# Every second tile of the ada stream on GpSimd, in a sum of its own

## Chip, cores, metric

The kernel runs on 1 core of one Trainium2 chip. The metric is the device time of one execution in microseconds (us), from which the median of several runs is taken. The core has five engines with a queue each: TensorE (PE in the profile; its weight loads are PEld), VectorE (DVE), ScalarE (ACT), GpSimd (POOL) and SyncE (SP), which here only issues DMAs.

## The reference

One layer of a decoder: 512 tokens of width 2048, in float32. A vector `c` gives, through one large matrix, six rows of 2048 values that shift, scale and gate the two halves of the layer:

```python
mod = (silu(c) @ w_ada + b_ada)                 # w_ada: 2048 x 12288
sh_a, sc_a, gt_a, sh_f, sc_f, gt_f = split(mod, 6)
h = rms_norm(x, g_attn) * (1 + sc_a) + sh_a
y = parallel_mixers(h, ...)                     # one projection w_in, two attentions, two gates, w_o
x = x + gt_a * y
h = rms_norm(x, g_ffn) * (1 + sc_f) + sh_f
x = x + gt_f * conv_ffn(h, ...)                 # w_up, 3-tap causal convolution, silu gate, w_down
```

Mixer A is an attention over the 128 keys that an indexer selects for each query; mixer B is a dense causal attention with latent projections (w_mq_up, w_mkv_up). Their outputs go through w_pa and w_pb, are multiplied by the sigmoids of the two gates, added, and go through w_o.

## The kernel before

**Products.** Every weight is used as two parts, high and low (`split`, lines 137 to 139, and `wtile`, lines 117 to 135): ScalarE rounds the float32 tile to its high part, VectorE subtracts that from the tile for the low part, and TensorE makes three products for each pair of operands (`mm3`, lines 141 to 144). A weight tile is 128 x 1024 in most places. It arrives in one of 5 buffers of `raw` by a DMA of SyncE's queue; its two parts stand in one of 3 pairs of buffers of `whl`. Part of the gates, nearly all of w_up, and w_down are multiplied by a scheme of seven products of halves instead of eight (`seven`, lines 948 to 1085; its matmuls are lines 1077 to 1079, its additions of weights line 973, its additions out of PSUM line 985).

**The ada stream.** The first two rows of `mod` are made at the start (`ada_units`). The other four, 8192 values, are made beside all the work from the mixer's attention to w_o, by `ada_stream` (lines 727 to 758), a generator. It has 16 blocks of 512 columns. A block has 16 tiles of 128 x 512 of `w_ada`; each is multiplied by one column of `c_act` (a scalar for each partition) and added to the block's sum `acc`, one of three tiles. One step of the generator handles a pair of tiles. The work around it asks for steps by a `ticker`: a rate for each stage (one step per weight tile in the gates beside attention A, 0.36 per step of the seven products, 1.25 per weight tile in w_pa, w_pb and w_o).

**Where a tile lands.** The load of a pair goes, in SyncE's queue, to one of three places: two tiles of the common pool (attention A and the gates; line 736), a `raw` buffer of the weights (from the first w_mkv_up to the last w_pa; line 740), or a ring of six pool tiles (w_pb and w_o; line 736 too). The pool has 81 tiles of 128 x 512 (`get`, `put`); a tile is given back as soon as the instructions that use it are recorded, and the next user waits for them. SyncE's queue is worked off in order.

**The end of a block.** `pend` keeps the finished sums. `flush_cols` (lines 780 to 797) splits each, adds its 128 partitions by two matmuls with a matrix of ones (lines 785 and 786) and stores the row or takes its columns. It is called at the beginning of a block of products, or when a sum is over three steps old.

**Order.** The kernel is recorded in one order; a scheduler of the build then orders the instructions of each engine by its own estimates and priorities (the loads and splits of weights have a high one). So an edit can move instructions that it doesn't touch.

**GpSimd before.** It issues the DMAs that store and reload attention outputs and gates (lines 713, 714, 807, 808, 827, 1108, 1109, 1274 to 1276), fills a few tiles with zeros (line 1169), and makes the power -0.5 of the norms, on 1 to 4 columns (`rsqrt_mean`, line 246).

Of the kernel before, what the change touches and what calls it, by code (L numbers as in the profile page):

```python
# [15 lines left out]
ALU = mybir.AluOpType  # L16
# [15 lines left out]
def trunk_layer_kernel(  # L32
# [21 lines left out]
    V, A, G, PE, SP = nc.vector, nc.scalar, nc.gpsimd, nc.tensor, nc.sync  # L54
# [14 lines left out]
    def get(dt=F32):  # L69

        i = min(free, key=lambda n: rested[n])
        free.remove(i)
        if cur[i] is None or cur[i].dtype != dt:
            cur[i] = pool.tile([P, T], dt, name=f"slot{i}", tag=f"slot{i}")
        held[id(cur[i])] = i
        return cur[i]
# [4 lines left out]
    def put(*ts, lag=2):  # L81

        for t in ts:
            i = held.pop(id(t))
            rested[i] = clock[0] + lag
            free.append(i)
# [146 lines left out]
    c_act = pool.tile([P, KD], F32, name="c_act")  # L233
# [312 lines left out]
    for tb in range(1, 4):  # L546
# [12 lines left out]
        acc = get()  # L559
        rl = [get(), get(), get()]  # L560
        for hd in range(16):
# [9 lines left out]
            else:  # L571
                V.scalar_tensor_tensor(acc[:, :S], r[:, :S], wi[:, tb, hd:hd + 1], acc[:, :S],  # L572
                                       op0=ALU.mult, op1=ALU.add)
# [146 lines left out]
    ada_blocks = [8, 9, 10, 11, 16, 17, 18, 19, 12, 13, 14, 15, 20, 21, 22, 23]  # L720
    gst = [get(), get()]
    ada_acc = [get(), get(), get()]

    ada_in_slots = [False]
    ada_ring_on, ada_ring = [False], deque()

    def ada_stream():
        for n, cb in enumerate(ada_blocks):
            assert len(pend) < 3
            acc = ada_acc[n % 3]  # L730
            for kp in range(8):
                if ada_in_slots[0]:
                    ts = [ada_ring.popleft(), ada_ring.popleft()] if ada_ring else [get(), get()]
                    for i in range(2):
                        k = kp * 2 + i
                        SP.dma_start(ts[i], w_ada[k * P:(k + 1) * P, cb * 512:(cb + 1) * 512])
                else:
                    raw = rawq.popleft()
                    t = raw[:, 0:1024].rearrange("p (k n) -> p k n", k=2)
                    SP.dma_start(t, w_ada[kp * 2 * P:(kp + 1) * 2 * P, cb * 512:(cb + 1) * 512]  # L740
                                 .rearrange("(k p) n -> p k n", p=P))
                    ts = [t[:, 0], t[:, 1]]
                for i in range(2):
                    k = kp * 2 + i
                    if k == 0:
                        V.tensor_scalar(acc, ts[i], c_act[:, 0:1], None, op0=ALU.mult)
                    else:
                        V.scalar_tensor_tensor(acc, ts[i], c_act[:, k:k + 1], acc,  # L748
                                               op0=ALU.mult, op1=ALU.add)
                if ada_ring_on[0]:  # L750
                    ada_ring.extend(ts)
                elif ada_in_slots[0]:
                    put(*ts)
                else:
                    rawq.append(raw)
                yield None
            pend.append((cb, acc))
            done[0] += 1

    pend = []  # L760
    done = [0]
    stream = ada_stream()

    credit = [0.0]
# [326 lines left out]
    for i in range(KH // 2):  # L1091
        raw = [get() for _ in range(4)]
        ta, tb_ = get(), get()
        for j in range(2):
            k, o = 2 * i + j, slice(j * HT, (j + 1) * HT)
# [334 lines left out]
    def up_group(grp):  # L1430
        gt = []

        def ev_g(m, b):
            t = conv(grp * 4 + m, b)
            A.activation(t, t, AF.Silu)
            gt.append(t)

        bk = half()
        flush_cols(bk[3])
        lin_fm(w_up, grp * 512, h2, KD, bk, ev_g, tick=sum_tick)  # L1440

        def ev_v(m, b):
            t = conv(44 + grp * 4 + m, b)
            V.tensor_tensor(t, t, gt[m], ALU.mult)
            f_out(grp * 4 + m, t)
            put(gt[m])

        lin_fm(w_up, 512 + grp * 512, h2, KD, half(), ev_v, tick=sum_tick)

    put(*ada_acc)  # L1450
    up_group(0)

    def ffn_out(i):
# [186 lines left out]
```

## Time and profile before

| | |
|---|---|
| median of 3 runs | 2657.04 us (2654.15 to 2658.64) |
| profiled execution | 2656.78 us, its span 2655.0 us |
| TensorE busy | 2588.7 us, 98% |
| VectorE busy | 2174.6 us, 82% |
| ScalarE busy | 1243.0 us, 47% |
| GpSimd busy | 365.8 us, 14% |

The profile is of one execution. The span runs from its first instruction to its last. An engine is busy while one of its instructions runs; waiting and issuing DMAs from SyncE is not counted, and TensorE's matmuls overlap, so that its busy time is the time in which at least one runs. In a row of a group, the number behind x is the count, the next the busy time in us, then the mean ns of one, then the engine's idle time just before, and who ended it. In a row of waits stand the waiting engine and line, an arrow to what it waited for, the us in total, the times and the longest. In a row of the timeline stand the start in us from the span's beginning, the duration in us, engine, line, operation, tiles and shapes.

### The profile page before, as it was taken

How to read it: one execution, taken by the hardware profiler on the slowest of the kernel's cores; microseconds unless marked ns; L12 is line 12 of the kernel's file. 1: busy time of each engine (PE TensorE's matmuls, PEld its weight loads, DVE VectorE, ACT ScalarE, POOL GpSimd, SP SyncE). 2: the span in 40 equal slices, each digit the busy share in tenths (PEclk: the TensorE clock that was granted, in tenths of full speed). 3: DMA queues.
4: the chain of work that ended last, by engine and by line, in shares of the span. 5: the costliest groups of instructions: out<-in, count | busy, mean ns of one | idle time of the engine just before them, and what ended most of it. 6: DMA issues, size and time to landing. Idle time of an engine off the chain costs nothing.

```text
span 2655.0 us, 44904 instructions
## 1 busy us (share of the span) xinstructions
PE 2588.7 (98%) x17168; PEld 2344.2 (88%) x17168; DVE 2174.6 (82%) x3491; ACT 1243.0 (47%) x1953; POOL 365.8 (14%) x671
## 2 busy tenths in 40 slices
PE   6999999999999999999999999999999999999999
PEld 5777687778998877888789999999999999999999
DVE  7886975779878786983669899899899889878787
ACT  4333434334445544322544555555555556655454
POOL 1000011010023223200100000000001024413120
PEclk8999899999999999999999999999999999999999
DMA  9953136774676489873324434433434447867563
GB/s 342 340 165 101 35 101 192 224 215 150 203 240 190 153 274 354 299 238 95 135 74 143 135 124 129 137 123 129 136 123 150 142 146 217 219 155 202 143 208 114
DMA packets 215661, 464.31 MB, mean 175 GB/s; under 512 B 23786, under 2 KB 65156, under 8 KB 215444
## 3 DMA queue, kind: packets, MB, share of 16 engines
q1 hardware_dynamic: 170260, 344.93, 40.4%
q0 software_dynamic: 45152, 116.50, 15.0%
q8 instruction: 134, 2.20, 0.3%
q14 instruction: 83, 0.68, 0.1%
q10 hardware_dynamic: 32, 0.01, 0.0%
HBM read 397.11 MB, written 64.23 MB: 174 GB/s over the span
## 4 chain that ended last, share of the span: by engine, by line
PE 80%; issue 7%; DMA 6%; DVE 5%; ACT 1%; POOL 1%; SPq 0%; POOLq 0%; DVEq 0%; ACTq 0%
PE bank L1077 15%; PE bank L1079 15%; PE bank L1078 15%; PE bank L142 10%; PE bank L143 10%; PE bank L144 10%; DMA slot<-in_w_ada 3%; DVE whl L139 1%; DMA x<-slot 1%; PE bank L708 1%; PE bank L903 1%; DVE slot L572 0%; DMA raw<-in_w_ada 0%; PE bank L700 0%; DMA slot<-in_x 0%
## 5 line engine op out<-in xcount | busy, mean ns | idle before, releaser
L1077 PE MATMUL bank<-slot,whl 128*128 128x256 f32 x3920 | 1102.7, 282 | 21.0 <-ACT slot L977 6.1
L1078 PE MATMUL bank<-slot,whl 128*128 128x256 f32 x3920 | 1098.9, 281 | 0.2 <-DVE slot L139 0.2
L1079 PE MATMUL bank<-slot,whl 128*128 128x256 f32 x3920 | 1088.2, 281 | 6.0 <-DVE whl L139 6.0
L138 ACT ACTIVATE whl<-raw 128x1024 fp32r<-128x1024 f32 (+2 forms) x560 | 532.6, 953 | 618.2 <-PE bank L1078 400.7
L1077 PEld LDWEIGHTS bank<-slot,whl 128*128 128x128 f32 x3920 | 738.9, 189 | 28.2 <-ACT slot L977 8.6
L1078 PEld LDWEIGHTS bank<-slot,whl 128*128 128x128 f32 x3920 | 740.1, 189 | 0.6 <-DVE slot L139 0.5
L1079 PEld LDWEIGHTS bank<-slot,whl 128*128 128x128 f32 x3920 | 732.3, 188 | 7.2 <-DVE whl L139 7.2
L139 DVE TENSOR_TENSOR whl<-raw,whl 128x1024 fp32r<-128x1024 f32 (+2 forms) x560 | 606.0, 1087 | 121.2 <-ACT whl L138 116.9
L130 ACT ACTIVATE whl<-raw 128x1024 fp32r<-128x1024 f32 (+4 forms) x182 | 187.3, 1031 | 385.6 <-PE bank L144 193.8
L973 DVE TENSOR_TENSOR raw<-raw 128x1024 f32<-128x1024 f32 (+2 forms) x320 | 347.3, 1085 | 6.7 <-DMA raw<-in_w_ups 3.7
L131 DVE TENSOR_TENSOR whl<-raw,whl 128x1024 fp32r<-128x1024 f32 (+4 forms) x182 | 215.8, 1186 | 163.7 <-ACT whl L130 162.7
L143 PE MATMUL bank<-whl,slot 128*128 128x512 f32 (+2 forms) x768 | 297.3, 388 | 0.9 <-DVE whl L131 0.9
L142 PE MATMUL bank<-whl,slot 128*128 128x512 f32 (+2 forms) x768 | 293.1, 393 | 4.3 <-ACT slot L409 3.8
L144 PE MATMUL bank<-whl,slot 128*128 128x512 f32 (+2 forms) x768 | 292.9, 385 | 0.0
L142 PE MATMUL bank<-slot,whl 128*128 128x512 f32 (+1 forms) x656 | 264.1, 407 | 6.2 <-DVE slot L703 3.8
L143 PE MATMUL bank<-slot,whl 128*128 128x512 f32 (+1 forms) x656 | 266.0, 406 | 0.1
L144 PE MATMUL bank<-slot,whl 128*128 128x512 f32 (+1 forms) x656 | 258.0, 402 | 0.0
L748 DVE SCALAR_TENSOR_TENSOR slot<-slot,c_act,slot 128x512 f32<-128x512 f32 x203 | 150.9, 747 | 46.0 <-DMA slot<-in_w_ada 44.4
L142 PEld LDWEIGHTS bank<-whl,slot 128*128 128x128 f32 x768 | 146.0, 190 | 35.6 <-ACT slot L409 3.9
L143 PEld LDWEIGHTS bank<-whl,slot 128*128 128x128 f32 x768 | 146.3, 191 | 30.0 <-DVE whl L131 1.4
L144 PEld LDWEIGHTS bank<-whl,slot 128*128 128x128 f32 x768 | 144.7, 189 | 29.4 <-issue 0.5
L142 PEld LDWEIGHTS bank<-slot,whl 128*128 128x128 f32 (+1 forms) x656 | 123.7, 189 | 37.2 <-DVE slot L703 4.2
(288 smaller groups left out, 2705.5 us busy)
## 6 DMA issues: line engine op xcount, KB each, us to landing
slot<-in_w_ada SPq DMA_DIRECT2D x344, 256.0 KB, 5.4
raw<-in_w_ups SPq DMA_DIRECT2D x160, 512.0 KB, 5.1
raw<-in_w_in SPq DMA_DIRECT2D x50, 512.0 KB, 3.7
raw<-in_w_down SPq DMA_DIRECT2D x64, 384.0 KB, 3.8
raw<-in_w_down SPq DMA_DIRECT2D x64, 320.0 KB, 3.1
slot<-f POOLq DMA_DIRECT2D x154, 128.0 KB, 4.1
f<-slot POOLq DMA_DIRECT2D x66, 256.0 KB, 5.1
raw<-in_w_gs SPq DMA_DIRECT2D x32, 512.0 KB, 3.9
```

The lines of the kernel that those rows point to most:

```text
L130: A.activation(hi, raw[:, :w], AF.Copy)
L131: V.tensor_tensor(lo, raw[:, :w], r32(hi), ALU.subtract)
L138: A.activation(dst_hi, src, AF.Copy)
L139: V.tensor_tensor(dst_lo, src, r32(dst_hi), ALU.subtract)
L142: PE.matmul(o, lh, rh, start=first, stop=False)
L143: PE.matmul(o, lh, rl, start=False, stop=False)
L144: PE.matmul(o, ll, rh, start=False, stop=last)
L748: V.scalar_tensor_tensor(acc, ts[i], c_act[:, k:k + 1], acc, op0=ALU.mult, op1=ALU.add)
L973: V.tensor_tensor(o[:, :W], a[:, :W], b[:, :W], op)
L1077: PE.matmul(o, wh[:, ks], rh, start=first and k == 0, stop=False, skip_group_check=True)
L1078: PE.matmul(o, wh[:, ks], rl, start=False, stop=False, skip_group_check=True)
L1079: PE.matmul(o, wl[:, ks], rh, start=False, stop=last, skip_group_check=True)
```

## The change

In each pair of tiles the second one goes to GpSimd. GpSimd multiplies it by its scalar, in place, and adds it to a sum of its own, `acc_g`; the first odd tile of a block is multiplied straight into `acc_g`. VectorE keeps the first tile of each pair with its fused multiplication and addition. At the end of a block VectorE adds `acc_g` to `acc`. There are two tiles `acc_g`, used in turn and taken from the pool with the other sums, given back with them.

```diff
     ada_acc = [get(), get(), get()]
+    ada_acc_g = [get(), get()]
...
-            acc = ada_acc[n % 3]
+            acc, acc_g = ada_acc[n % 3], ada_acc_g[n % 2]
...
                 for i in range(2):
                     k = kp * 2 + i
-                    if k == 0:
-                        V.tensor_scalar(acc, ts[i], c_act[:, 0:1], None, op0=ALU.mult)
+                    if i:
+                        G.tensor_scalar(ts[i] if kp else acc_g, ts[i], c_act[:, k:k + 1], None, op0=ALU.mult)
+                        if kp:
+                            G.tensor_tensor(acc_g, acc_g, ts[i], ALU.add)
+                    elif kp == 0:
+                        V.tensor_scalar(acc, ts[i], c_act[:, k:k + 1], None, op0=ALU.mult)
                     else:
                         V.scalar_tensor_tensor(acc, ts[i], c_act[:, k:k + 1], acc,
                                                op0=ALU.mult, op1=ALU.add)
...
+            V.tensor_tensor(acc, acc, acc_g, ALU.add)
             pend.append((cb, acc))
...
-    put(*ada_acc)
+    put(*ada_acc, *ada_acc_g)
```

The multiplication of GpSimd is line 748 of the changed kernel, its addition line 750, VectorE's first and other tiles lines 752 and 754, the addition of the two sums line 763; the lines behind are shifted by seven, those ahead of line 722 not at all.

## Prediction

> **What bounds the kernel now.** I read the engines' shares and the chain that ended last first, then the busy time by stretches, cut where the work around the ada stream changes, then what TensorE waited for.
>
> ```profile
> span 2655.0 us, 44904 instructions
> ...
> PE 2588.7 (98%) x17168; PEld 2344.2 (88%) x17168; DVE 2174.6 (82%) x3491; ACT 1243.0 (47%) x1953; POOL 365.8 (14%) x671
> ...
> PE 80%; issue 7%; DMA 6%; DVE 5%; ACT 1%; POOL 1%; SPq 0%; POOLq 0%; DVEq 0%; ACTq 0%
> ```
>
> TensorE bounds the kernel. VectorE, which the change relieves, is second, and 5% of the chain. GpSimd is nearly idle.
>
> ```profile
> core 0: us, PE busy (x) PEld busy (x) DVE busy (x) ACT busy (x) POOL busy (x), PEclk, DMA share, GB/s
> 440.00:590.00 150.00, 150.00 (x671) 116.41 (x670) 116.16 (x252) 55.68 (x115) 13.97 (x26) 1.00 0.71 222
> 590.00:660.00 70.00, 64.22 (x415) 57.77 (x414) 64.33 (x95) 29.42 (x41) 4.84 (x9) 0.95 0.52 169
> 660.00:790.00 130.00, 126.66 (x1044) 125.56 (x1044) 108.22 (x124) 54.39 (x71) 17.27 (x33) 0.99 0.66 208
> 790.00:960.00 170.00, 169.57 (x831) 138.47 (x830) 132.11 (x408) 87.04 (x193) 46.49 (x69) 1.00 0.61 189
> 960.00:1060.00 100.00, 95.12 (x402) 72.25 (x401) 75.18 (x141) 40.85 (x76) 30.58 (x57) 0.97 0.98 345
> 1060.00:1200.00 140.00, 140.00 (x602) 112.78 (x602) 121.06 (x173) 48.02 (x69) 18.96 (x32) 1.00 0.78 259
> 1200.00:1330.00 130.00, 126.97 (x573) 102.67 (x573) 66.08 (x98) 50.19 (x77) 9.62 (x17) 0.99 0.33 114
> ```
>
> The second column is TensorE's busy time, the fourth VectorE's, the sixth GpSimd's. The ada stream runs from 440 to 1200 us. In those six stretches TensorE is idle for 0 + 5.8 + 3.3 + 0.4 + 4.9 + 0 = 14.4 us. No relief of VectorE can bring more than that: 0.54% of the time. The waits of TensorE from 440 to 1330 us say whose fault it was:
>
> ```profile
> PE bank L142 <- DVE slot L703: 3.8, 1, 3.8
> PE bank L1077 <- ACT slot L138: 3.5, 1, 3.5
> PE bank L1079 <- DVE whl L139: 3.3, 2, 2.7
> PE bank L1077 <- ACT slot L826: 2.1, 1, 2.1
> PE bank L700 <- DVE slot L692: 0.9, 1, 0.9
> ```
>
> The two waits of L1077 (5.6 us) fall at the start of the gate products in halves, where VectorE is 92% busy (64.33 of 70) making their operands; L139 is VectorE's half of the split of weights. So VectorE is the limit for some 9 us, around 590 to 790 us. The 3.8 us of L703 is a copy out of PSUM in the attention's end.
>
> **What leaves VectorE.**
>
> ```profile
> L748 DVE SCALAR_TENSOR_TENSOR slot<-slot,c_act,slot 128x512 f32<-128x512 f32 x203 | 150.9, 747 | 46.0 <-DMA slot<-in_w_ada 44.4
> L139 DVE TENSOR_TENSOR slot<-slot,slot x148: 406/683/694, 474.0 to 2543.4; 128x512 fp32r<-128x512 f32 x134, 128x256 fp32r<-128x256 f32 x14
> ```
>
> The stream has 16 blocks of 16 tiles. The 8 odd tiles of each go: 128 x 0.747 = 95.6 us. One add of two 128x512 tiles per block comes, at the 0.683 us median of the like-shaped split: 16 x 0.683 = 10.9 us. VectorE loses 84.7 us, almost all of it where TensorE has work anyway.
>
> **What GpSimd gets.** 128 multiplications, 112 additions of 128x512; no such operation is in the trace. The nearest rows:
>
> ```profile
> L1169 POOL MEMSET slot<- 64x512 f32 x8 | 4.2, 524 | 9.4 <-PE bank L1209 5.7 <-PE bank L1078 2.2 <-PE bank L1213 0.7
> masks.py:199 POOL TENSOR_SCALAR_AFFINE_SELECT ident<-ident 128x128 f32<-128x128 f32 x1 | 0.3, 312 | 0.1
> L192 POOL MEMSET mhalf<- 128x4 f32 x1 | 0.1, 102 | 0.0
> ```
>
> A fill of 512 columns takes 0.52 us; that is the lower end for one input. The select reads and writes 128 columns in 0.312 us, 0.102 of it the fixed cost of the smallest fill; for 512 columns 0.10 + 4 x 0.21 = 0.94 us is the upper end. I take 0.75, between them, as the select compares too. An addition reads twice: 0.10 + 2 x 0.42 = 0.94 us from the fill, 0.10 + 2 x 0.84 = 1.78 us from the select; I take 1.2, nearer the fill, since most of a select's price is not its reading. An odd tile then costs GpSimd 1.95 us (1.46 to 2.72) where VectorE paid 0.75. In all 128 x 0.75 + 112 x 1.2 = 230 us, on an engine with time for it.
>
> The Trainium skill, "GPSIMD Engine Reference", section 3.1, has about 2.6 cycles per element at 1.2 GHz for two inputs, by which I estimate 512 x 2.6 / 1.2 = 1.1 us for an addition; the sum would be nearly the same.
>
> **What that does to VectorE.** GpSimd's only reading operation in the stream's time is the small power L246, and the trace shows it beside VectorE's splits:
>
> ```profile
> 817.83 0.70 POOL L246 TENSOR_TENSOR rs<-rsm,mhalf 128x2 f32<-128x2 f32 x1 [1.70 <-DVE rsm L245]
> 805.18 0.95 DVE L131 TENSOR_TENSOR whl<-raw,whl 128x768 fp32r<-128x768 f32 x1
> 805.34 1.33 POOL L246 TENSOR_TENSOR rs<-rsm,mhalf 128x2 f32<-128x2 f32 x1 [0.59 <-DVE rsm L245]
> 813.49 1.21 DVE L131 TENSOR_TENSOR whl<-raw,whl 128x1024 fp32r<-128x1024 f32 x1
> 813.65 1.82 POOL L246 TENSOR_TENSOR rs<-rsm,mhalf 128x2 f32<-128x2 f32 x1 [6.39 <-DVE rsm L245]
> ```
>
> Alone the power takes 0.70 us. Started inside a split it takes 1.33 and 1.82 us: the first ends 0.54 us behind its split (806.67 against 806.13). The two engines do not read at the same time: GpSimd stood until VectorE's operation was over. That VectorE also stands while GpSimd reads cannot be seen here, as two columns take no time. Bounds for VectorE: nothing (84.7 us gained), or the whole of GpSimd's 230 us wherever VectorE's operation reads two tiles in SBUF, as the splits, the subtractions L973 and the stream's own L748 do.
>
> The Trainium skill, "SBUF — State Buffer", section "Who interferes with whom", says that such a pair of operations excludes each other for a whole instruction, whichever started first; the trace agrees for GpSimd's side (1.33 and 1.82 against 0.70 us), and no run here shows VectorE's.
>
> I take the upper bound in the gate products and less elsewhere. The stream's operations by stretch (in the same stretches as above; 16 of TENSOR_SCALAR form come on top, so odd tiles are 8/15 of the count):
>
> ```profile
> 440.00:590.00 150.00, 43.70 (x59) 1.00 0.71 222
> 590.00:660.00 70.00, 11.88 (x16) 0.95 0.52 169
> 660.00:790.00 130.00, 20.97 (x28) 0.99 0.66 208
> 960.00:1060.00 100.00, 32.67 (x44) 0.97 0.98 345
> 1060.00:1200.00 140.00, 44.68 (x60) 1.00 0.78 259
> ```
>
> - 590 to 660 us: 8.5 odd tiles. VectorE 64.3 - 8.5 x 0.747 + 0.7 for one add = 58.7; with GpSimd's 8.5 x 1.95 = 16.6 one after the other 75.3 us, in a stretch of 70. VectorE sets the pace there already: **+5 us**.
> - 660 to 790 us: 15 odd tiles. 108.2 - 11.2 + 1.4 + 29.3 = 127.7 of 130 us. The room falls from 22 to 2 us, and a split that comes late stops TensorE (L139, above): **+4 us**, between -3.3 (that wait goes) and +10.
> - 440 to 590 us: 31.5 odd tiles, 116.2 - 23.5 + 2.7 + 61.4 = 157 of 150 us if everything were excluded, but here many of VectorE's operations read PSUM or a single tile (the attention's minima, scalings and copies); TensorE never waited here, and weights are split ahead: 0.
> - 1060 to 1200 us: 32 odd tiles, 121.1 - 23.9 + 2.7 + 62.4 = 162 of 140, with 64 us of VectorE's idle time right behind it and TensorE full in both: 0.
> - 960 to 1060 us: 23.5 odd tiles are 46 us for GpSimd beside its 30.6 us, mostly DMA issues: 76% busy. Stores and reloads of attention outputs and gates stand behind additions that wait for their tile to land (98% of the DMA engines' time is taken here). TensorE already lost 4.9 us here: **+3 us**, from 0 to 8.
> - Relief: of the 9 us of waits on VectorE's load some goes: **-2 us**, at most -9.
>
> **The order of issue.** The stream's loads, the weights' loads and their waits share SyncE's queue (SyncE's waits from 440 to 1330 us; the first row is of the DMA issues).
>
> ```profile
> slot<-in_w_ada SPq DMA_DIRECT2D x344, 256.0 KB, 5.4
> SPq L736 <- DVE slot L748: 86.7, 129, 3.5
> SPq L126 <- DVE whl L131: 226.5, 67, 20.7
> ```
>
> The two new sums take two tiles of the common pool. In the built order the first 70 tile loads of the stream go round three buffers instead of five, and half of these loads wait for GpSimd. A buffer turns in 5.4 us of landing and 0.75 or 1.95 of use: 6.75 on the mean, through three buffers 2.25 us per tile; the stream takes 150 / 63 = 2.4 today (59 x 16/15 = 63 tiles in the first stretch). It just fits. Weights behind it have cover: L126 waits for splits, 226.5 us in all, so it runs as far ahead as its buffers let it. Late sums have cover too:
>
> ```profile
> 464.47 0.75 DVE L748 SCALAR_TENSOR_TENSOR slot<-slot,c_act,slot 128x512 f32<-128x512 f32 x1
> 486.80 0.69 PE L785 MATMUL bank<-slot,ones_r 128*128 128x512 f32 x1
> ```
>
> Block 1 is summed at 465.2 us and TensorE takes it up at 486.8, 21.6 us later; its place in TensorE's built order hardly moves. One add (0.7 us) and GpSimd's last tile (1.95) fit in.
>
> **Sum.** +5 + 4 + 3 - 2 = +10 us on the profiled execution's 2656.78 us (span 2655.0), 0.3 us below the median of 2657.04: **2667 us**.
>
> **Rivals.**
> 1. *It helps.* GpSimd's reading does not hold VectorE. Then VectorE's 84.7 us are a gift, and the waits of L1077 and L139 go: 5.6 + 3.3 = 8.9 us, perhaps less: 2649 to 2651, say 2650. For it: those waits are real, and no VectorE row is stretched. Against: the power's rows. It decides from GpSimd holding VectorE for under 0.75 us per odd tile. Chance 0.17.
> 2. *No difference.* Cover takes up both signs, as TensorE has 98%: 2657, within 5.3 us. About 0.2% is what a measurement of this kernel can tell from no change. Chance 0.20.
> 3. *SyncE's queue becomes the bound.* If each GpSimd operation stands behind one 1.2 us split, an odd tile takes 1.95 + 2.4 = 4.35 us; three buffers at 5.4 + 2.55 give 2.65 us per tile, 63 tiles 167 us instead of 150, and in the gate products late weights follow late tiles: 17 us and the 10 above less some overlap, 2680. For it: the 1.82 us row, where two VectorE operations in a row kept GpSimd out. Against: weights run ahead. Chance 0.18.
>
> **Numbers.** The forecast, 2662.5 to 2674, has 0.45. Faster is rival 1, 0.17; same rival 2, 0.20; slower the forecast and rival 3, 0.63. The range reaches over rival 1's middle and most of rival 3: 2650 to 2685.
>
> **What would show it.** Right: L748 under POOL at about 0.75 and 1.2 us, more beside splits; the splits L139 and L131 (shifted lines) longer than 1.22 us for 1024 columns; more TensorE idle time between 590 and 790 us and near 1000. Wrong: splits unstretched; or TensorE's loss lies in another stretch, above all behind 1330 us, where the change has no instruction; or SyncE waits for GpSimd by tens of us and weights land late.

## The result and the profile after

The changed kernel takes 2728.38 us (median of 4 runs, 2726.84 to 2732.4), the kernel before 2657.84 us beside it. The ratio is 1.0268, with a 95% interval of 1.0253 to 1.0283: 70.5 us slower. The forecast was 10 us slower, and its range ended at 2685. The sign was right, the size was wrong by 60 us.

The page of the changed kernel, with its span, its engines and its chain:

```profile
span 2726.5 us, 44994 instructions
...
PE 2613.6 (96%) x17168; PEld 2361.9 (87%) x17168; DVE 2184.2 (80%) x3379; ACT 1244.5 (46%) x1953; POOL 783.1 (29%) x911
...
PE 69%; DVE 10%; DMA 9%; issue 6%; POOL 4%; ACT 1%; SPq 0%; DVEq 0%; POOLq 0%; ACTq 0%
```

VectorE was to lose 84.7 us of work and is busy for 9.6 us more than before (2174.6): the operations it kept became 94 us longer in all. TensorE has the same 17168 matmuls, stands idle for 46.6 us more, and is busy for 24.9 us more.

Where the time went is read from stretches cut at the same points of the work in both kernels: the first and last of the seven products of the gates, the first w_mkv_up, the last product of attention B's keys, the output x1, the first seven products of w_up. The windows of the kernel before, then those of the changed one (columns as in the prediction):

```profile
440.00:615.50 175.50, 173.39 (x772) 135.02 (x770) 139.93 (x291) 65.15 (x128) 16.66 (x31) 1.00 0.68 212
615.50:788.60 173.10, 166.09 (x1350) 163.55 (x1351) 147.81 (x178) 73.71 (x99) 18.02 (x34) 0.97 0.63 200
788.60:807.00 18.40, 18.40 (x94) 16.45 (x94) 12.62 (x40) 9.89 (x25) 11.18 (x19) 1.00 1.00 326
807.00:1020.50 213.50, 212.96 (x1007) 168.66 (x1006) 170.49 (x472) 98.09 (x212) 56.02 (x90) 1.00 0.68 221
1020.50:1286.60 266.10, 261.34 (x1114) 209.36 (x1113) 174.22 (x242) 89.22 (x131) 30.22 (x53) 0.99 0.65 221
1286.60:1389.90 103.30, 100.28 (x459) 81.32 (x458) 75.79 (x119) 53.81 (x82) 9.62 (x17) 0.98 0.32 108
1389.90:2655.00 1265.10, 1242.69 (x10417) 1236.11 (x10415) 1113.26 (x1402) 682.31 (x996) 189.20 (x320) 1.00 0.50 151
```

```profile
440.00:629.90 189.90, 177.88 (x777) 136.85 (x775) 134.65 (x254) 65.48 (x131) 120.38 (x95) 0.98 0.65 203
629.90:822.20 192.30, 172.71 (x1350) 169.23 (x1351) 154.53 (x172) 75.36 (x102) 90.52 (x72) 0.94 0.55 178
822.20:846.60 24.40, 24.00 (x122) 21.13 (x121) 17.33 (x56) 13.65 (x33) 14.89 (x21) 1.00 0.87 285
846.60:1063.00 216.40, 202.54 (x942) 157.58 (x941) 163.47 (x414) 92.02 (x200) 134.03 (x126) 0.99 0.60 192
1063.00:1354.20 291.20, 275.67 (x1152) 218.97 (x1152) 183.40 (x221) 92.50 (x134) 186.43 (x153) 0.97 0.65 219
1354.20:1457.20 103.00, 100.03 (x460) 81.26 (x459) 75.82 (x119) 54.19 (x82) 9.74 (x17) 0.98 0.31 108
1457.20:2726.50 1269.30, 1244.54 (x10417) 1237.91 (x10415) 1113.42 (x1402) 682.07 (x996) 189.56 (x320) 1.00 0.50 150
```

The rest of attention A and the plain gates: +14.4 us. The gates' seven products: +19.2, with the same 1350 matmuls. The next three stretches, from the end of the seven products to x1, have to be read together: the scheduler moved matmuls across the cuts between them (94, 1007 and 1114 before, 122, 942 and 1152 after), but their sum is the same within one. They took 498.0 us and take 532.0: +34.0. Behind them -0.3 and +4.2. So about half of the loss lies between the seven products and x1, where the prediction had +3 in all.

The loss shows in two forms. TensorE's idle time grew: from 2.1 to 12.0 us in the first stretch, from 7.0 to 19.6 in the second, from 5.3 to 29.8 in the next three. And with it the granted clock fell: from 0.97 to 0.94 in the seven products, where the same matmuls are busy for 172.7 us and not 166.1. VectorE's room is not used up: in the seven products it works 154.5 of 192.3 us.

What GpSimd's operations take (the rows of their lines in the changed kernel whose tiles are all in the pool, without the 20 and 17 operations on `raw` buffers: shortest, median, longest in ns):

```profile
L748 POOL TENSOR_SCALAR slot<-slot,c_act x108: 1552/1586/6021, 432.2 to 1302.0; 128x512 f32<-128x512 f32 x108
L750 POOL TENSOR_TENSOR slot<-slot,slot x95: 1257/1304/4106, 441.8 to 1304.9; 128x512 f32<-128x512 f32 x95
```

Even the shortest multiplication takes 1.55 us, twice the 0.75 taken and far above the upper end of 0.94. An addition of two tiles is cheaper, 1.30 us in the median.

The two engines hold each other up. VectorE's groups in the changed kernel, and its split of weights in the kernel before (first row):

```profile
L131 DVE TENSOR_TENSOR whl<-raw,whl 128x1024 fp32r<-128x1024 f32 (+4 forms) x182 | 215.8, 1186 | 163.7 <-ACT whl L130 162.7 <-PE bank L144 0.7
```

```profile
L131 DVE TENSOR_TENSOR whl<-raw,whl 128x1024 fp32r<-128x1024 f32 (+4 forms) x182 | 222.7, 1225 | 144.9 <-ACT whl L130 144.7
...
L754 DVE SCALAR_TENSOR_TENSOR slot<-slot,c_act,slot 128x512 f32<-128x512 f32 x95 | 90.6, 953 | 70.9 <-DMA slot<-in_w_ada 70.3
```

The stream's own fused operation takes 953 ns on the mean where it took 747. The timeline shows both sides, first VectorE behind GpSimd:

```profile
553.38 1.41 POOL L750 TENSOR_TENSOR slot<-slot,slot 128x512 f32<-128x512 f32 x1
553.55 2.31 DVE L131 TENSOR_TENSOR whl<-raw,whl 128x1024 fp32r<-128x1024 f32 x1
```

The split, some 1.22 us by itself, started 0.17 us into the addition and ended 1.07 us behind it (555.86 against 554.79): nearly its whole length. Then GpSimd behind VectorE (the row of line 748 in a short window, and VectorE's first and last operations there):

```profile
L748 POOL TENSOR_SCALAR slot<-slot,c_act x2: 3377/4659/5941, 572.3 to 575.6; 128x512 f32<-128x512 f32 x2
```

```profile
575.20 0.74 DVE L754 SCALAR_TENSOR_TENSOR slot<-slot,c_act,slot 128x512 f32<-128x512 f32 x1
...
579.47 0.69 DVE L1104 TENSOR_TENSOR slot<-slot,slot 128x512 f32<-128x512 f32 x1
```

The multiplication that started at 575.6 took 5.94 us. VectorE ran eight operations on two tiles back to back until 580.16; GpSimd's ended 1.4 us after the last of them, about its own length.

And the waits of the changed kernel from 430 to 1360 us: SyncE's for GpSimd, VectorE's for GpSimd's sum, and TensorE's three largest and the one for the second half of a sum's split (L793).

```profile
SPq L737 <- POOL slot L750: 128.6, 48, 9.7
...
SPq L126 <- POOL slot L750: 24.5, 10, 4.8
```

```profile
DVE slot L763 <- POOL slot L750: 17.7, 6, 5.6
```

```profile
PE bank L1084 <- ACT slot L986: 9.8, 4, 6.8
PE bank L792 <- ACT slot L138: 6.8, 3, 4.9
PE bank L1084 <- ACT slot L138: 6.5, 1, 6.5
...
PE bank L793 <- DVE slot L139: 4.3, 3, 2.4
```

SyncE's wait ahead of weight loads for VectorE's splits, in the same window, before and after:

```profile
SPq L126 <- DVE whl L131: 261.7, 74, 20.7
```

```profile
SPq L126 <- DVE whl L131: 149.7, 62, 7.3
```

SyncE's queue, which loads the weights and the stream, now stands for GpSimd: 128.6 us ahead of loads of the stream, and 24.5 us ahead of weight loads (L126) that go into `raw` buffers whose tile GpSimd read. In the kernel before the largest wait of that queue for the stream's consumer was 86.7 us in 129 short pieces. These waits are not lost time by themselves. From 440 us to x1 the rows of SyncE's waits add up to 715 us of 846.6 before and 769 of 914.2 after, 84% both times: where SyncE stands longer for the stream, it stands shorter for the splits.

L1084 is the first matmul line of the seven products, L792 and L793 are the two matmuls of the stream's own sums: operands and sums come late. Of TensorE's waits from 440 us to x1 (14 us before, 61 after, by the sums of their rows), those for parts of weights are 3.3 and 9.4 us. The rest, 11 and 52 us, is for operands that ScalarE and VectorE made.

### The profile page after: what moved, and what is told of

Its sections match the earlier page's. It is cut to its first block, busy times and chain, and to the rows that moved or that the text cites. A ratio compares the mean times of both kernels' runs of the same rounds, so it can differ in the third digit from the quotient of the medians.

```text
span 2726.5 us, 44994 instructions
## 1 busy us (share of the span) xinstructions
PE 2613.6 (96%) x17168; PEld 2361.9 (87%) x17168; DVE 2184.2 (80%) x3379; ACT 1244.5 (46%) x1953; POOL 783.1 (29%) x911
## 4 chain that ended last, share of the span: by engine, by line
PE 69%; DVE 10%; DMA 9%; issue 6%; POOL 4%; ACT 1%; SPq 0%; DVEq 0%; POOLq 0%; ACTq 0%
PE bank L1084 13%; PE bank L1085 13%; PE bank L1086 13%; PE bank L142 9%; PE bank L144 9%; PE bank L143 9%; DMA slot<-in_w_ada 5%; POOL slot L748 2%; DMA x<-slot 1%; DVE whl L139 1%; DMA raw<-in_w_ada 1%; DVE slot L754 1%; POOL slot L750 1%; DVE raw L980 1%; DVE slot L139 1%
## 5 line engine op out<-in xcount | busy, mean ns | idle before, releaser
L1084 PE MATMUL bank<-slot,whl 128*128 128x256 f32 x3920 | 1108.2, 284 | 37.1 <-ACT slot L986 13.5
L1084 PEld LDWEIGHTS bank<-slot,whl 128*128 128x128 f32 x3920 | 742.1, 189 | 44.6 <-ACT slot L986 15.0
L139 DVE TENSOR_TENSOR whl<-raw,whl 128x1024 fp32r<-128x1024 f32 (+2 forms) x560 | 613.7, 1102 | 121.9 <-ACT whl L138 118.0
L980 DVE TENSOR_TENSOR raw<-raw 128x1024 f32<-128x1024 f32 (+2 forms) x320 | 353.1, 1104 | 7.9 <-DMA raw<-in_w_ups 3.7
L131 DVE TENSOR_TENSOR whl<-raw,whl 128x1024 fp32r<-128x1024 f32 (+4 forms) x182 | 222.7, 1225 | 144.9 <-ACT whl L130 144.7
L748 POOL TENSOR_SCALAR slot<-slot,c_act 128x512 f32<-128x512 f32 x108 | 214.2, 1987 | 169.9 <-DMA slot<-in_w_ada 139.9
```

The costliest lines, as they stand in the source:

```text
L131: V.tensor_tensor(lo, raw[:, :w], r32(hi), ALU.subtract)
L139: V.tensor_tensor(dst_lo, src, r32(dst_hi), ALU.subtract)
L748: G.tensor_scalar(ts[i] if kp else acc_g, ts[i], c_act[:, k:k + 1], None, op0=ALU.mult)
L980: V.tensor_tensor(o[:, :W], a[:, :W], b[:, :W], op)
L1084: PE.matmul(o, wh[:, ks], rh, start=first and k == 0, stop=False, skip_group_check=True)
```

## Experiments

All times are medians; the difference is to the kernel before in the same series.

| run | what it is | us | difference | ratio, 95% interval |
|---|---|---|---|---|
| changed kernel | | 2728.38 | +70.5 | 1.0268 (1.0253 to 1.0283) |
| e1 | before, two pool tiles held | 2678.44 | +18.9 | 1.0067 (1.0052 to 1.0082) |
| e2 | e1, GpSimd reads beside | 2725.51 | +65.9 | 1.0242 (1.0227 to 1.0258) |
| e3 | e1, GpSimd writes beside | 2683.91 | +24.3 | 1.0087 (1.0071 to 1.0102) |
| e4 | every fourth tile on GpSimd | 2708.98 | +49.4 | 1.0184 (1.0166 to 1.0201) |
| e5 to e8 | in one stage alone: A, S, B, W | 2682.28, 2684.65, 2689.63, 2684.91 | +22.5, +24.8, +29.8, +25.1 | 1.0086 to 1.0113 (each within 0.0022) |
| e9 | multiplication on ScalarE | 2717.04 | +59.3 | 1.0217 (1.0201 to 1.0233) |
| e10 | one GpSimd sum, one tile more | 2714.01 | +56.2 | 1.0212 (1.0198 to 1.0227) |
| e11 | odd tiles not held | 2691.23 | +33.5 | 1.0135 (1.011 to 1.0159) |
| e12 | before, one pool tile more | 2652.12 | -5.7 | 0.9982 (0.9973 to 0.9991) |
| e13 | no final addition | 2712.89 | +54.1 | 1.02 (1.0185 to 1.0215) |
| e14 | odd loads from GpSimd's queue | 2755.47 | +96.6 | 1.0369 (1.0352 to 1.0386) |
| e15 | ring of 12 | 2722.51 | +63.7 | 1.0241 (1.0224 to 1.0258) |
| e16 | e11 without GpSimd | 2669.64 | +10.4 | 1.0047 (1.0031 to 1.0064) |
| e17 | GpSimd on 64 of 512 columns | 2712.20 | +52.9 | 1.0204 (1.0187 to 1.0221) |
| e18 | e17 without the final addition | 2696.46 | +38.0 | 1.0147 (1.0129 to 1.0165) |

**The parts laid on the kernel before (e1 to e3).** The first theory was turns: the loss is VectorE and GpSimd excluding each other. Its rival: tiles and sums come late, or the two tiles are missed. e1 takes only the tiles:

```diff
+    kept = [get(), get()]
...
-    put(*ada_acc)
+    put(*ada_acc, *kept)
```

> The kernel before, with two more tiles of the pool taken where the change takes its two sums, and nothing computed in them. Theory 'turns' (VectorE and GpSimd exclude each other while both read tiles in SBUF, and VectorE's operations stand behind GpSimd's): within 5 us of before. Theory 'late tiles' (odd tiles are held longer, the loads behind them in SyncE's queue come late): within 5 us too, as VectorE gives tiles back after 0.75 us. Theory 'two tiles less' (the pool is too small then): a good part of the 70 us, 20 or more.

+18.9 us for two tiles that nothing touches, well above what the first two theories allowed and near the third. The prediction had no term for them.

e2 adds GpSimd's two reading operations on a tile of its own, started by VectorE; VectorE sums all tiles as before. e3 puts five fills of about the same total length in their place.

```diff
+                    if i:
+                        s = kept[0][:, n * 8 + kp:n * 8 + kp + 1]
+                        with tc.issue_after(v.ins):
+                            V.memset(s, 0.0)
+                        G.tensor_scalar(kept[1], kept[1], s, None, op0=ALU.mult)
+                        if kp:
+                            G.tensor_tensor(kept[1], kept[1], kept[1], ALU.add)
```

> e1, and beside each odd tile GpSimd does the change's two operations (128x512, one with a scalar, one of two tiles) on a tile of its own, started by a tiny VectorE fill behind the odd tile's own VectorE operation. VectorE still sums all tiles, so nothing waits for GpSimd's values. 'Turns': as much as the change or more, since VectorE keeps its 85 us of work: 65 to 110 us over e1, VectorE's 1024-column splits up to 2.3 us. 'Late tiles': within 8 us of e1, as tiles go back as before. A full GpSimd queue (DMAs and norms behind the arithmetic): 20 to 70 us, like e3.

> e2 with five fills of 128x512 (0.52 us each, 2.6 us in all) in place of the two reading operations (2.8 us): GpSimd's queue is as full, but it reads no tile. 'Turns': within 8 us of e1, splits at 1.22 us. 'Late tiles': within 8 us of e1. A full GpSimd queue: about as slow as e2. If writing excludes VectorE too: about as slow as e2, with the splits stretched.

The engines' busy time in e1; then that of e2 with the row of its split of weights (shortest, median, longest); then the same two of e3:

```profile
PE 2594.2 (97%) x17168; PEld 2347.5 (88%) x17168; DVE 2176.7 (81%) x3491; ACT 1243.7 (46%) x1953; POOL 369.6 (14%) x671
```

```profile
PE 2612.8 (96%) x17168; PEld 2355.0 (87%) x17168; DVE 2276.1 (84%) x3620; ACT 1242.8 (46%) x1953; POOL 758.5 (28%) x911
```

```profile
L131 DVE TENSOR_TENSOR whl<-raw,whl x182: 806/1219/2532, 34.2 to 1439.1; 128x1024 fp32r<-128x1024 f32 x134, 128x1104 fp32r<-128x1104 f32 x16, 128x896 fp32r<-128x896 f32 x16, 128x640 fp32r<-128x640 f32 x8
```

```profile
PE 2597.7 (97%) x17168; PEld 2347.3 (87%) x17168; DVE 2186.2 (81%) x3620; ACT 1243.6 (46%) x1953; POOL 710.2 (26%) x1439
```

```profile
L131 DVE TENSOR_TENSOR whl<-raw,whl x182: 806/1220/1311, 33.8 to 1401.4; 128x1024 fp32r<-128x1024 f32 x134, 128x1104 fp32r<-128x1104 f32 x16, 128x896 fp32r<-128x896 f32 x16, 128x640 fp32r<-128x640 f32 x8
```

GpSimd is about as busy in both, and ahead of its own DMA issues in both. Reading costs 47 us above e1, and VectorE is busy for 99 us more, of which some 10 are the small fills that start GpSimd (they are in e3 too); writing costs 5.5 us and stretches no split. So a full GpSimd queue is cheap, and reading beside VectorE is dear as long as VectorE keeps all its work, though less dear than the 65 to 110 us that "turns" had.

The Trainium skill, "SBUF — State Buffer", section "Who interferes with whom", says that an operation of VectorE with two inputs in SBUF contends with a GpSimd instruction that reads SBUF, and not with one that only writes it. Both runs agree: splits of up to 2.53 us beside reads, 1.31 us at most beside fills.

**Less of the change (e4 to e8).** e4 gives GpSimd only the odd tiles of every second pair (`if i and kp % 2`); e5 to e8 use GpSimd in one stage alone and leave the rest as before, with a flag set where the stage begins: A, the rest of attention A and the gates; S, the gates' seven products and what follows up to the `raw` buffers; B, the loads through `raw`; W, w_pb and w_o.

```diff
-                    if i:
+                    if i and stage[0] in ON:
```

> The change for every fourth tile instead of every second: 64 tiles on GpSimd, 64 x 2.8 = 180 us of it. 'Turns': 15 to 35 us over before, half of the change's loss or less, as VectorE has room where it is not full. 'Late tiles': 30 to 40 us, half.

> The change only in the steps recorded beside attention A and the first gates (63 of 256 tiles there, half on GpSimd); elsewhere VectorE takes all tiles. 'Turns': 5 to 15 us over before, lost where the sums for the seven products are made. 'Late tiles' (three buffers there): 10 to 25 us.

> The change only in the steps recorded in the gates' seven products, where VectorE does almost nothing but operations on two tiles and is 85% busy. 'Turns': 15 to 25 us over before. 'Late tiles': under 8 us, as a step is asked for only every 8 us there.

> The change only in the steps recorded beside mixer B and w_pa, where tiles land in the weights' buffers. 'Turns': 3 to 15 us over before. 'Late tiles': 5 to 15 us, as a weight's buffer is held 3 us longer.

> The change only in the steps recorded in w_pb and w_o (ring of six tiles). 'Turns': 15 to 25 us over before. 'Late tiles': 20 to 35 us, with sums late at TensorE. If the losses of the four stretches add up, e5 to e8 come to about 70 us in all.

Half the tiles cost 70% of the loss, more than either theory had. But e4 still has the two tiles (18.9 us in e1) and all 16 final additions (some 16 us, e13 below). Without these two parts, 15 of 36 us stay, which fits a price per tile.

Of the stages alone, e5 came out where "late tiles" had it, e6 where "turns" had it, e8 where the two meet, and e7 (+29.8, where no theory had more than 15) in neither. Above e1 the four cost 3.6, 5.9, 10.9 and 6.2 us: with e1's 18.9 that makes 45.5, and some 25 us of the 70.5 appear only when the stages follow each other (a sum of many differences, uncertain by some 15 us, going by the intervals). Prices of single stages, added up, fall short of the change.

**Faster or fewer (e9, e10, e12).** e9 multiplies on ScalarE (0.72 us a tile) and leaves GpSimd the addition. e10 has one GpSimd sum and a pool of 82 tiles, made room for by smaller small buffers, so that as many tiles are free as in the kernel before. e12 is the kernel before with that pool of 82.

```diff
-                        G.tensor_scalar(ts[i] if kp else acc_g, ts[i], c_act[:, k:k + 1], None, op0=ALU.mult)
+                        A.activation(ts[i] if kp else acc_g, ts[i], AF.Copy, scale=c_act[:, k:k + 1])
```

```diff
-    n_slots=81,
+    n_slots=82,
...
-    sm = ctx.enter_context(tc.tile_pool(name="small", bufs=6))
+    sm = ctx.enter_context(tc.tile_pool(name="small", bufs=5))
...
-        tmp = sm.tile([P, 2, H, rot], F32, name="ropetmp", bufs=2)
+        tmp = sm.tile([P, 2, H, rot], F32, name="ropetmp", bufs=1)
```

> The change with the odd tile's multiplication on ScalarE (in place, about 0.6 us) and only its addition on GpSimd: GpSimd reads for 1.28 us per odd tile instead of 2.83. 'Turns' (47 us in e2 over e1): that part falls to some 20 to 30, so 40 to 50 us over before, with the 19 us of the two tiles in it. If GpSimd's time does not matter, as slow as the change.

> The change with a single tile for GpSimd's sum, and the pool grown by one tile to 82 (small buffers 5 deep instead of 6, the rotation's temporary 1 instead of 2), so that the rest has as many tiles as before. If the 19 us of e1 are the lack of tiles: 45 to 55 us over before. If they are something else: as slow as the change.

> The kernel before with the pool grown to 82 tiles by the same small buffers as in e10, no work on GpSimd. If tiles are what the stream lacks: 2 to 10 us faster than before. If 81 are enough and 79 too few: within 5 us.

e9 takes more than half of GpSimd's work away and wins only 11 us, less than "turns" had. e10 gives the tiles back and wins 14, near what e1 had measured for them, though with one sum GpSimd cannot begin a block before the final addition of the last one. Neither the price of GpSimd nor the tiles carry most of the loss. e12 is faster than before by 5.7 us, as expected if tiles are what the stream lacks: one tile more is worth something to the kernel as it was, and e12 is the fastest version here.

**Who waits for GpSimd (e11, e13 to e15).** e11 leaves the odd tiles out of the sum. They are loaded, their slots are free on landing, and GpSimd makes its two operations on a tile of its own as in e2; VectorE has lost its half of the stream and adds nothing at the end, so nobody waits for GpSimd's values.

> The change with VectorE's half of the sum alone: odd tiles are loaded and left out of the sum, their buffers free on landing; GpSimd does the same two operations on a tile of its own, started by VectorE's even tile. VectorE is relieved, GpSimd as busy, nobody waits for GpSimd's values. 'Turns': within 10 us of the change, 58 to 72 us over before. 'Late tiles': at least 25 us less than the change, 45 us over before or under.

It recovers 37 us with turns still taken, as "late tiles" had it. So about half of the loss is waiting and the final addition. e13 to e15 ask for which wait: e13 drops the final addition (the odd tiles are left out of the result), e14 issues the odd tiles' loads from GpSimd, e15 has twice the ring.

```diff
-            V.tensor_tensor(acc, acc, acc_g, ALU.add)
```

```diff
-                        SP.dma_start(ts[i], w_ada[k * P:(k + 1) * P, cb * 512:(cb + 1) * 512])
+                        (G if i else SP).dma_start(ts[i], w_ada[k * P:(k + 1) * P, cb * 512:(cb + 1) * 512])
```

```diff
-    ada_ring.extend(get() for _ in range(6))
+    ada_ring.extend(get() for _ in range(12))
```

> The changed kernel without VectorE's addition of GpSimd's sum to its own at the end of a block (the odd tiles are so left out of the result; GpSimd still multiplies and adds them and holds their buffers as long). Nothing on VectorE or TensorE then waits for GpSimd's sum. Theory (a), the tiles that GpSimd still holds make SyncE's queue stand, and what loads behind them lands late: the wait of SyncE's L737 for L750 (128.6 us in the change) stays above 100 us and the time stays within 8 us of the change's 2728. Theory (b), the sums are late, because VectorE waits in order for GpSimd's sum (L763, 17.7 us) with TensorE's sums behind it: at most half of the 37 us that are open stays, so 2690 to 2710. Dropping 16 additions of 0.78 us alone is worth at most 12 us of VectorE's time, of which TensorE would see a part.

> The changed kernel with the loads of the odd tiles, outside the gate phase with the raw buffers, issued from GpSimd's own queue and not from SyncE's. SyncE then never stands there for a tile that GpSimd holds; the tile's new load is late instead, and nobody's other load with it. Theory (a), the standing queue: the wait of SyncE's L737 for L750 falls from 128.6 us to under 20 us, and the time by 15 to 37 us, to 2691 to 2713. Theory (b), late sums: the time stays within 8 us of 2728 or is above it, since some 90 issues more stand in GpSimd's order ahead of its additions.

> The changed kernel with twelve tiles in the stream's ring where there are six, in the stage of w_pb and w_o (which grew from 266.1 to 291.2 us). A tile then has twice the time to come free. Theory (a): SyncE's wait for L750 inside this stage falls by more than half, and the time by 10 to 20 us, to 2708 to 2718. Theory (b), or turns alone: within 8 us of 2728, since sums are as late and GpSimd's operations as slow. Six tiles fewer in the pool in that stage would by themselves cost some us, going by the 18.8 us of two tiles over the whole stream.

e13 recovered 16 us, between the two theories, and SyncE stood nearly as long (its wait in e13):

```profile
SPq L737 <- POOL slot L750: 115.8, 51, 5.9
```

e14 was a failed experiment: it came out where the second theory had it, above the change, but for a reason of its own making. It did not take the wait away, since even tiles are loaded into slots that odd ones held, and it put 108 issues into GpSimd's queue that stood there for other engines, 89.8 us in all (SyncE's wait in e14, then the group of the new issues, whose idle time stands behind the second bar):

```profile
SPq L737 <- POOL slot L750: 112.2, 30, 13.7
```

```profile
L737 POOL DMA_DIRECT2D slot<-in_w_ada x108 | 61.6, 571 | 89.8 <-DVE slot L754 35.8 <-DVE slot L139 16.4 <-DVE slot L752 11.6
```

e15 won 6 us, within what late sums or turns alone had. Its ring did what it was to do: from 1060 to 1360 us SyncE's wait for L750 is 32.3 us instead of 62.0. The 10 to 20 us of the first theory did not come back with it, so in this stage SyncE's standing does not seem to be where most of the time goes, though the six tiles that the ring takes from the pool may hide a part.

**How long GpSimd holds, or that it holds at all (e16 to e18).** e16 is e11 without any GpSimd operation. e17 is the change with GpSimd's operations on 64 of 512 columns (the other columns of the odd tiles are left out of the result, and VectorE fills the two sums with zeros once); every tile, wait and addition stands. e18 drops the final addition from e17.

```diff
-                        G.tensor_scalar(ts[i] if kp else acc_g, ts[i], c_act[:, k:k + 1], None, op0=ALU.mult)
+                        G.tensor_scalar((ts[i] if kp else acc_g)[:, :64], ts[i][:, :64], c_act[:, k:k + 1], None, op0=ALU.mult)
                         if kp:
-                            G.tensor_tensor(acc_g, acc_g, ts[i], ALU.add)
+                            G.tensor_tensor(acc_g[:, :64], acc_g[:, :64], ts[i][:, :64], ALU.add)
```

> The kernel of e11 without any operation of GpSimd: two tiles held, the odd tiles loaded and left out of the result, their buffers free on landing, VectorE with half the stream's operations. What e11 (+33.5 us) has above this is the price of taking turns alone, with VectorE's relief in both. Theory 'turns': the price is what it was without relief (47 us from e1 to e2), so this comes out at 2658 + 33.5 - 47, some 2645, 10 to 15 us faster than before though two tiles are missing. Theory 'tiles': relief is worth little here, and this stays near 2658 + 19 = 2677 (2670 to 2680), so that turns were only some 15 us in e11.

> The changed kernel with GpSimd's two operations on 64 of a tile's 512 columns (the other columns of the odd tiles are so left out of the result). Every wait, queue, tile and addition of the change stands, but GpSimd holds an odd tile for well under half as long, and shares an eighth of the reading. Theory 'GpSimd's duration': time falls to the price of two tiles less VectorE's relief plus 16 additions, 2650 to 2685, and SyncE's wait for L750 (128.6 us) to under 40 us. Theory 'the order itself' (any engine more that must release a tile makes SyncE's queue stand, and any wait for a second sum delays the first): it stays above 2705, with SyncE's wait over 80 us.

> e17 without VectorE's final addition (odd tiles multiplied and added on 64 of 512 columns, and left out of the result). e17 lies 42 us above e16, which differs from it by who releases the odd tiles and by the final addition and its wait. Theory 'held tiles': the order in which GpSimd, in its queue behind landings and DMA issues, releases odd tiles is what costs; the final addition is worth what it was in e13, 16 us, so 2694 to 2700. Theory 'late sums': with GpSimd's work short, the wait for its sum was the larger part, so 2670 to 2682.

e16 came out at the lower edge of what "tiles" had (2670 to 2680), some 25 us above "turns".

e17's rows of GpSimd's two lines (shifted by two), and its waits for GpSimd's tiles by SyncE and ScalarE:

```profile
L750 POOL TENSOR_SCALAR slot<-slot,c_act x108: 432/461/4607, 432.3 to 1194.1; 128x64 f32<-128x64 f32 x108
```

```profile
L752 POOL TENSOR_TENSOR slot<-slot,slot x95: 307/325/1337, 437.8 to 1194.7; 128x64 f32<-128x64 f32 x95
```

```profile
SPq L739 <- POOL slot L752: 67.1, 54, 5.9
```

```profile
ACT slot L138 <- POOL slot L752: 24.7, 5, 7.8
```

An odd tile now costs GpSimd 0.46 + 0.33 = 0.79 us, about what VectorE paid (0.75), and three quarters of the loss stay. SyncE's wait fell to 67.1 us, above the one theory's 40 and below the other's 80; the time, above 2705, is the second theory's. e18 came out where "held tiles" had it (2694 to 2700). What its GpSimd does between operations is the row of its waits:

```profile
POOL slot L750 <- DMA slot<-in_w_ada: 216.6, 71, 9.3
```

GpSimd stands 216.6 us for tiles to land, with its stores and reloads behind. SyncE, in contrast, waits alike in e16 and e18: from 430 to 1360 us the rows of its waits add up to 781.0 and 781.6 us, those ahead of the stream's loads on pool tiles to 283.8 and 298.8. And TensorE waits for parts of weights for 1.4 and 0.5 us. So the 27.6 us between these two runs do not show as late weights.

## Where the 70.5 us went

Two chains of runs, each step with one thing more, by differences of medians:

| | through short operations | through untouched tiles |
|---|---|---|
| two tiles fewer, VectorE's relief | 10.4 (e16) | 10.4 (e16) |
| odd tiles go through GpSimd's queue | 27.6 (e18 - e16) | 20.6 (e13 - e11) |
| final addition and its wait | 14.9 (e17 - e18) | 16.4 (changed - e13) |
| full length of GpSimd's reading | 17.6 (changed - e17) | 23.1 (e11 - e16) |
| sum | 70.5 | 70.5 |

Every entry is uncertain by some 6 us, going by the intervals. The two ways agree within that about the addition and the reading, and nearly about the tiles. Part of the second row may be something else: e18 has GpSimd's short operations, which e16 lacks, and e11 has VectorE's small fills (9.5 us of its time in e3), which e13 lacks.

So no one part carries the loss; four do, of 10 to 28 us each. The second row is not an engine's arithmetic. In the kernel before, one engine took both tiles of a pair in the order of their loads; now a second queue has to come round to every odd tile, and that queue also issues stores and stands for landings. By which way this reaches TensorE stays open. It does not show as late weights (e16 and e18 above). ScalarE's waits for slots that GpSimd read (24.7 us in e17) and GpSimd's late stores are left, and were not taken apart. e11 and e16 free the odd slots even sooner than the kernel before did, so the first row may be a few us too low and the second too high.

## Why the prediction was wrong

By its own steps:

1. **What bounds the kernel: held.** No relief of VectorE could bring more than 14.4 us, rival 1 said 8.9. e16 against e1: 18.9 - 10.4 = 8.5 us for 96 us of VectorE's work, with odd slots freed on landing.
2. **What GpSimd gets: mis-sized.** 1.59 and 1.30 us where 0.75 and 1.2 were taken, so 128 x 1.586 + 112 x 1.304 = 349 us and not 230. The multiplication lies outside its bounds. The fill and the select that gave them have no second operand for each partition; whether that makes the difference, no run shows. The size is worth part of the 18 to 23 us, not the rest: e17 ran below the predicted price and was 53 us slower than before.
3. **What that does to VectorE: the mechanism held, the size lay between the bounds.** VectorE's operations did become longer beside GpSimd's reading, by 94 us. That is more than the whole relief, but well under the upper bound of 230 us, or 349 with the measured operations.
4. **The stretches: failed.** "+5, +4, 0, 0, +3" compared VectorE's work with its room. The gates' two stretches, +9 in the prediction, came to +19.2 with 38 us of VectorE's time unused. In 440 to 590 us, "weights are split ahead: 0", lie some 10 of the first +14.4: the matmuls made by 590 us in the kernel before are made by 600 in the changed one. Between the seven products and x1 the prediction had +3 for 960 to 1060 us, 0 for w_pb and w_o ("64 us of VectorE's idle time right behind it"), and no term for 790 to 960 us, where 33 of the stream's operations lie; the stretch cost 34.0. VectorE had room throughout, so a sum of its work could not show the loss.
5. **The order of issue: failed, with the next two the main miss.** "It just fits" (2.25 us per tile through three buffers) counted landing and GpSimd's own time, not the time until GpSimd's queue comes round. The runs show 20.6 to 27.6 us for it. That an odd tile comes free late was in rival 3. But rival 3 priced it at 17 us and tied it to GpSimd standing behind splits and to late weights: the cost is there with operations of 0.79 us too, and "weights behind it have cover" largely held (TensorE's waits for them rose from 3.3 to 9.4 us).
6. **Late sums have cover: failed.** 21.6 us of lead for block 1 was taken for all blocks. TensorE waits 6.8 + 4.3 = 11.1 us for splits of the stream's sums, against 0.5 us at most in the kernel before; the final addition and its wait cost 15 to 16 us. VectorE's own time for the 16 additions is 12.5 us (16 x 0.781); how much of the 15 to 16 is this and how much lateness was not taken apart.
7. **Two tiles of the pool: named, never priced.** 18.9 us (e1), nearly twice the whole forecast, for a line that served only to count buffers.
8. **Nothing was set down for the clock.** 24.9 us of the loss are busy time of the same matmuls, at a granted clock of 0.982 against 0.990 over the span. By the clock alone 2588.7 us would become some 2610, an estimate of 21 us. It fell as TensorE's stalls grew, but not by their sum alone: with 91.5 us of idle time e11 had 0.989, with 93.1 us e17 had 0.984.

The chances had 0.63 on slower, which came. The direction rested on stretched VectorE operations, which were there; that it came with three parts that the sum had at nothing is not to its credit. The range failed since these parts were missing, and since the others were taken as separate: e5 to e8 show that stages cost more in a row than one by one. That a late tile makes the next stage's sums and slots late would explain it, and was not shown.

## What to carry to other kernels

Before giving every second tile to another engine, ask not only what that engine takes for a tile, but when its queue comes round to it, what else stands in that queue, and who waits for the tile's release: here that cost about as much as the slower arithmetic, and cutting the arithmetic to an eighth of the columns won back only a quarter of the loss. Price the buffers that a second sum takes by holding them in the old kernel with nothing in them: two of 81 tiles were 18.9 us, and one tile more was worth 5.7. A long wait of a queue is not a loss by itself: SyncE waited 84% of the time in both kernels, and halving one of its waits (e15) won little. Where the bounding engine is 98% busy, as here, relief of another engine can win only the bounding engine's waits.

## What the hardware showed

- GpSimd multiplied a 128x512 float32 tile by a scalar for each partition in 1.55 us at best, longer than it took to add two tiles (1.26). The Trainium skill, "GPSIMD Engine Reference", section 3.1, gives 769 ns measured for 512 elements in a tight loop, as the best case; the row is twice that, and for this operation the row decides. Its two-input figure, by which an addition was estimated at 1.1 us, was near.
- On 64 columns the two took 0.46 and 0.33 us, from which, with the medians on 512 columns, I estimate about 0.3 and 0.2 us fixed and 2.5 and 2.2 ns for each column.
- VectorE's operations on two tiles, one right behind the other, can keep a GpSimd read out for several of them: 5.94 us for an operation of 1.55.
